# A hybrid attention and mixture-of-experts layer: the stretch from the output projection to the first expert rebuilt, the first group's gather in one piece, the last down projection in its own PSUM bank, the final norm inside the branch

## The chip, the cores and the metric

The kernel runs on one core of a Trainium2 chip. The metric is the device time of one execution in microseconds (us), as the median of the runs of one kernel. Engines are named as in the profile: PE (TensorE), DVE (VectorE), ACT (ScalarE), POOL (GpSimd) and SP (SyncE, which issues most DMA transfers).

## The reference, cut to what matters

256 tokens of width 1024, all float32. Three attention branches give a gated sum `merged`; what follows is where the change lies:

```python
x = layer_norm(DEEPNORM_ALPHA * x + merged @ w_o, ln1_g, ln1_b)      # x1
# router: 4 groups of 4 experts; best group, then its best 2 experts, for every token
p_grp = softmax(t @ w_rg + b_rg);  p_top, g_idx = top_k(p_grp, 1)
sel = take_along_axis((t @ w_re + b_re).reshape(256, 4, 4), g_idx)
pe_top, e_idx = top_k(softmax(sel), 2);  w_tok = p_top * pe_top / sum(pe_top)
for e in range(16):
    h = silu(t @ w1[e]) * (t @ w3[e])          # 1024 -> 512
    out += combine[:, e:e+1] * (h @ w2[e])     # 512 -> 1024
x = layer_norm(DEEPNORM_ALPHA * x + out, ln2_g, ln2_b)
```

## The kernel before

**Stages.** Projections and the three branches fill the first part of the execution. Then come the output projection (8 weight tiles `i`, into four PSUM banks `z[t][half]` for two token tiles `t` of 128 tokens and two column halves), the first layer norm with the router, 16 experts, and the last layer norm with the store.

**First norm and router.** x1 is normalised in place in `xt`, with gamma and beta: `x1_dve` does a half on DVE alone (`L961`, `L963`), `x1_pool` does one by an activation on ACT (`L966`) and a multiplication and an addition on POOL (`L967`, `L968`). x1 is then split into a high part `x1h` (ACT, `L972`) and a remainder `x1l` (`L976`, on DVE or POOL), since PE multiplies in a reduced-precision form of float32 and two products restore the accuracy. The router takes its logits from the sums before normalisation: `pre_T` transposes them (the copies are `L915`), `raw_logits` multiplies, `logits` (`L928` to `L931`) turns the products into `L` with the mean and the reciprocal deviation. DVE ranks the logits by all pairwise comparisons (`L1037` to `L1047`, ties by the mask `lower`), PE counts the places within an expert (`L1055` and around), and DVE makes the one-hot matrices `sel` that pick each expert's up to 64 tokens (`L1123`).

**Gather.** For each group of four experts the chosen tokens are multiplied out of x1h and x1l by `sel` (`L1142`, 8 matmuls for a bank, 4 banks), and ACT or DVE copies a bank to `xg` (`L1144`). For group 0 three banks stand ahead of expert 0's first up step and the fourth between its first and second.

**Experts.** Every expert has 4 up steps (`L1176`; two weight tiles of 512 KB, 8 matmuls), a copy by ACT (`L1181`), transposes, silu and product (`hidden`), and 4 down steps (`L1213`; one tile, 4 matmuls) into one PSUM bank `sd`, whose result goes out by ACT and DVE (`L1219`, `L1220`, the last expert's `L1223`, `L1224`). PE's order is written out in strings: `u` and `d` are steps, `x` is what lies between (the shape of the next hidden layer, and `scatter`, which adds a finished expert's rows into the four accumulators `acc`, `L1235` and `L1243`). The accumulators start from x1 times alpha by PE matmuls with a diagonal matrix (`acc_init`, `L990`).

**Weights.** SP issues one 512 KB transfer for each of the 192 expert tiles, always in order. A tile's target is one of 16 `raw` buffers or a half of a finished region that `W.lend` hands over (`lraw`). The next transfer into a buffer is issued when PE has used the tile in it, so the stream runs ahead as far as buffers are free: 39 tiles are issued before the first up step.

**End.** After the last scatter stands a branch for experts with more than 64 tokens, which is not taken with these inputs. Behind it every engine jumps over that block's code to the last norm (`L1367` to `L1394`: statistics on DVE for token tile 0, sums and squares on ACT for tile 1); four stores of 256 KB follow, issued by SP (`L1384`).

`warm(n)` issues n small matmuls whose result is not used, `WARM` has their numbers.

Of the kernel before, what the change touches and what calls it, by code (L numbers as in the profile page):

```python
# [41 lines left out]
WARM = (5, 8, 19)  # L42
FALLBACK = True
# [146 lines left out]
def tile_block(  # L190
# [159 lines left out]
    lower = consts.tile([128, 4, 4], F32, name="lower")  # L350
    nc.gpsimd.memset(lower, 1.0)
    nc.gpsimd.affine_select(out=lower, in_=lower, pattern=[[1, 4], [-1, 4]], compare_op=OP.is_gt, fill=0.0, base=0,
# [389 lines left out]
    def router_sums():  # L742
        b = bank("sd", None)
        nc.gpsimd.memset(junk, 1.0)
        for k in range(KC):
            nc.tensor.matmul(b[:, 0:40], junk, R["wrg"][:, k].rearrange("p a n -> p (a n)"), start=(k == 0),
                             stop=(k == KC - 1))
        wsum = R["wsum"]
        nc.vector.tensor_copy(wsum, b[:, 0:40].rearrange("p (a n) -> p a n", a=2))
        nc.vector.tensor_add(wsum[:, 1, :], wsum[:, 1, :], R["br"])  # L750
# [117 lines left out]
    def wo_mm(i, t):  # L868
        hi, lo = W.parts(nproj + i)
        hf = (i // 2) % 2  # L870
        for kk in range(2):
            k = 4 * (i // 4) + 2 * (i % 2) + kk
            ts = slice(t * 128, t * 128 + 128)
            for n, (w, a) in enumerate(((hi, R["oh"]), (lo, R["oh"]), (hi, R["ol"]))):
                nc.tensor.matmul(z[t][hf], a[:, k, ts], w[:, kk, :], start=(k == 0 and n == 0),
                                 stop=(k == KC - 1 and n == 2))

    class Stats:


        def __init__(self):
            self.st = small.tile([128, 2, 6], F32, name="lnst")
# [3 lines left out]
        def half(self, h, src):  # L886
            nc.vector.bn_stats(self.st[:, h, :], src)  # L887
# [5 lines left out]
        def shift(self):  # L893

            d = small.tile([128, 1], F32, name="shift")
            nc.vector.scalar_tensor_tensor(d, self.mv[:, 0:1], -1.0, self.rs, op0=OP.mult, op1=OP.mult)
            return d

# [3 lines left out]
    def ln1_half(s, t, h):  # L902

        v = xt[:, t, 512 * h:512 * h + 512]
        nc.vector.scalar_tensor_tensor(v, v, ALPHA, z[t][h], op0=OP.mult, op1=OP.add)
        s.half(h, v)
# [3 lines left out]
    def pre_T(t, h):  # L910
        b = bank("sd", (4, 128))
        for i in range(4):
            k = 4 * h + i
            nc.tensor.transpose(b[:, i, :], xt[:, t, k * 128:k * 128 + 128], ident)
        nc.scalar.copy(preT[:, 4 * h:4 * h + 4, t * 128:t * 128 + 128], b)  # L915

    def raw_logits(t, h):

        if h == 0:
            lb[t] = bank("sd", None)  # L920
        for k in range(4 * h, 4 * h + 4):
            nc.tensor.matmul(lb[t][:, 0:20], preT[:, k, t * 128:t * 128 + 128], wrg[:, k, 0, :], start=(k == 0),
                             stop=(k == KC - 1))

    def logits(t, s):

        nrs = small.tile([128, 1], F32, name="nrs")
        nc.vector.tensor_scalar(nrs, s.rs, -1.0, None, op0=OP.mult)  # L928
        q = small.tile([128, 20], F32, name="lq")
        nc.vector.scalar_tensor_tensor(q, wsum[:, 0, :], s.mv[:, 0:1], lb[t][:, 0:20], op0=OP.mult, op1=OP.subtract)  # L930
        nc.vector.scalar_tensor_tensor(L[:, t, :], q, nrs, wsum[:, 1, :], op0=OP.mult, op1=OP.add)  # L931
# [7 lines left out]
    nc.vector.tensor_scalar(junk, ident, ALPHA, None, op0=OP.mult)  # L939
# [13 lines left out]
    s0, s1 = Stats(), Stats()  # L953
    for h in range(2):
        ln1_half(s0, 0, h)
    s0.finish()
    d0, d1 = halves_of(x1[:, 0]), halves_of(x1[:, 1])

    def x1_dve(d, s, h, stage):
        if stage == 0:  # L960
            nc.vector.scalar_tensor_tensor(d[h], d[h], s.mv[:, 0:1], g1[h], op0=OP.subtract, op1=OP.mult)  # L961
        else:
            nc.vector.scalar_tensor_tensor(d[h], d[h], s.rs, b1[h], op0=OP.mult, op1=OP.add)  # L963

    def x1_pool(d, s, h, shift):
        nc.scalar.activation(d[h], d[h], AF.Identity, scale=s.rs, bias=shift)  # L966
        nc.gpsimd.tensor_mul(d[h], d[h], g1[h])  # L967
        nc.gpsimd.tensor_add(d[h], d[h], b1[h])  # L968

    def x1_hi(t, h):  # L970
        hs = slice(512 * h, 512 * h + 512)
        nc.scalar.copy(x1h[:, t, hs], x1[:, t, hs])  # L972

    def x1_lo(t, h, eng):
        hs = slice(512 * h, 512 * h + 512)
        eng.tensor_sub(x1l[:, t, hs], x1[:, t, hs], x1h[:, t, hs])  # L976

    def wo_last(i):
        wo_mm(i, 1)
# [4 lines left out]
    acc = [None, None]  # L984

    def acc_init(t):

        acc[t] = [bank("mm", None) for _ in range(2)]
        for h in range(2):
# [3 lines left out]
    pre_T(0, 1)  # L993
    shift0 = s0.shift()
    wo_last(5)
    x1_pool(d0, s0, 1, shift0)
    pre_T(0, 0)
    x1_dve(d0, s0, 0, 0)
    ln1_half(s1, 1, 0)
    x1_dve(d0, s0, 0, 1)  # L1000
    wo_last(6)
    raw_logits(0, 0)
    raw_logits(0, 1)
    pre_T(1, 0)
    wo_last(7)
    x1_hi(0, 0)
    x1_hi(0, 1)
    x1_lo(0, 1, nc.gpsimd)
    logits(0, s0)
    x1_lo(0, 0, nc.vector)  # L1010
    W.lend(0)
    W.lend(1)
    raw_logits(1, 0)
    warm(WARM[0])
    ln1_half(s1, 1, 1)
    s1.finish()
    pre_T(1, 1)
    raw_logits(1, 1)
# [409 lines left out]
```

## Time and profile before

| | |
|---|---|
| median of 3 runs | 663.99 us (663.24 to 665.48) |
| profiled execution | 665.7 us, of which the span of the trace is 664.0 us |
| mean granted clock of PE | 0.985 |
| busy, share of the span | PE 637.4 us (96%), DVE 350.9 (53%), ACT 282.9 (43%), POOL 40.1 (6%) |
| DMA | 176.59 MB, mean 266 GB/s |
| stream of expert weights | 393 to 395 GB/s in each of the 28th to the 37th of the page's 40 slices |

The span runs from the first to the last instruction or transfer in the trace; the time of the execution is a little longer. Times below are counted from the start of the span. A clock of 1.00 is 2.4 GHz, 0.50 is 1.2 GHz.

### The profile page before, as it was taken

What the parts mean: (1) busy time and instruction counts of PE and PEld (TensorE: products, weight loads), DVE (VectorE), ACT (ScalarE), POOL (GpSimd) and SP (SyncE); (2) the same over time, 40 slices, a digit from 0 to 9 for tenths busy, and PEclk for the clock granted to TensorE, in tenths of its full rate; (3) what the DMA queues carried; (4) which work ended last, traced back from release to release, by engine and by line L of the source; (5) the groups of instructions that cost most, each with busy time, mean ns of one, the idle gap of its engine ahead of it and who ended that gap; (6) DMA issues with size and microseconds to landing.
All of it is one profiled execution on the core that took longest, in us unless ns stands there. A gap on an engine that the chain in (4) does not pass through costs nothing. (4 is left out here: it accounts for less than half of the span.)

```text
span 664.0 us, 9601 instructions
## 1 busy us (share of the span) xinstructions
PE 637.4 (96%) x3645; PEld 463.9 (70%) x3645; DVE 350.9 (53%) x594; ACT 282.9 (43%) x487; POOL 40.1 (6%) x65
## 2 busy tenths in 40 slices
PE   6999999999999999999999999899999999999981
PEld 5899999898998888888998888534434433543320
DVE  4755657679888677776676676711122112111214
ACT  6654445466647555454345453312233223222212
POOL 2000000101001002100000002300000000000001
PEclk9999999999999999999999999899999999999987
DMA  8997444555445556797645768899999999999971
GB/s 271 378 386 271 148 143 156 159 149 169 139 148 173 164 159 201 244 342 276 193 166 185 251 191 280 321 314 394 394 394 394 393 394 395 394 394 394 390 264 68
DMA packets 84294, 176.59 MB, mean 266 GB/s; under 512 B 5856, under 2 KB 8320, under 8 KB 83984
## 3 DMA queue, kind: packets, MB, share of 16 engines
q1 hardware_dynamic: 83216, 172.14, 73.9%
q0 software_dynamic: 1024, 3.76, 1.9%
q8 instruction: 30, 0.49, 0.3%
q14 instruction: 24, 0.20, 0.1%
HBM read 174.83 MB, written 1.05 MB: 265 GB/s over the span
## 5 line engine op out<-in xcount | busy, mean ns | idle before, releaser
L131 DVE TENSOR_TENSOR lo_lo<-raw,hi_hi 128x1024 fp32r<-128x1024 f32 x118 | 144.3, 1224 | 92.4 <-ACT hi_hi L116 91.8
L116 ACT CAST hi_hi<-raw 128x1024 fp32r<-128x1024 f32 x118 | 123.2, 1047 | 127.7 <-PE mm L401 54.9
L388 PE MATMUL mm<-xh,hi_hi 128*128 128x256 f32 x320 | 91.8, 287 | 0.0
L388 PE MATMUL mm<-xh,lo_lo 128*128 128x256 f32 x320 | 90.5, 283 | 0.0
L388 PE MATMUL mm<-xl,hi_hi 128*128 128x256 f32 x320 | 90.5, 283 | 0.0
L1220 DVE SCALAR_TENSOR_TENSOR y_5b<-sd,cring,y_5b 64x512 fp32r<-64x512 f32 x30 | 22.5, 750 | 114.8 <-ACT y_5b L1219 114.8
L1176 PE MATMUL sd<-raw,xg 128*64 128x512 f32 x212 | 67.2, 596 | 0.0
L401 PE MATMUL mm<-hi_hi,xh 128*128 128x512 f32 x160 | 64.1, 401 | 0.0
L401 PE MATMUL mm<-hi_hi,xl 128*128 128x512 f32 x160 | 62.5, 391 | 0.0
L401 PE MATMUL mm<-lo_lo,xh 128*128 128x512 f32 x160 | 62.5, 390 | 0.0
L388 PEld LDWEIGHTS mm<-xh,hi_hi 128*128 128x128 f32 x320 | 61.3, 192 | 0.6
L388 PEld LDWEIGHTS mm<-xl,hi_hi 128*128 128x128 f32 x320 | 61.3, 192 | 0.1
L388 PEld LDWEIGHTS mm<-xh,lo_lo 128*128 128x128 f32 x320 | 61.3, 192 | 0.0
L1176 PE MATMUL sd<-lraw,xg 128*64 128x512 f32 x156 | 50.9, 596 | 0.9 <-ACT scratch L1181 0.9
L1181 ACT COPY scratch<-sd 128x512 f32<-128x512 f32 x16 | 9.4, 586 | 81.1 <-PE sd L1176 81.1
L1176 PEld LDWEIGHTS sd<-raw,xg 128*64 128x64 f32 x212 | 19.2, 137 | 29.2 <-issue 24.2
L401 PE MATMUL mm<-hi_hi,fh 128*128 128x512 f32 x96 | 37.9, 394 | 0.0
L401 PE MATMUL mm<-hi_hi,fl 128*128 128x512 f32 x96 | 37.5, 390 | 0.0
L401 PE MATMUL mm<-lo_lo,fh 128*128 128x512 f32 x96 | 37.4, 390 | 0.0
L401 PEld LDWEIGHTS mm<-hi_hi,xl 128*128 128x128 f32 x160 | 30.0, 188 | 6.5
L401 PEld LDWEIGHTS mm<-hi_hi,xh 128*128 128x128 f32 x160 | 30.1, 188 | 5.7
L401 PEld LDWEIGHTS mm<-lo_lo,xh 128*128 128x128 f32 x160 | 30.1, 188 | 5.5
(355 smaller groups left out, 1128.4 us busy)
## 6 DMA issues: line engine op xcount, KB each, us to landing
raw<-in_w_dram SPq DMA_DIRECT2D x80, 512.0 KB, 10.5
raw<-in_w_in_dram SPq DMA_DIRECT2D x75, 512.0 KB, 3.7
lraw<-in_w_dram SPq DMA_DIRECT2D x56, 512.0 KB, 10.6
raw<-in_w_branch_dram SPq DMA_DIRECT2D x24, 512.0 KB, 4.4
lraw_hi<-in_w_dram SPq DMA_DIRECT2D x18, 512.0 KB, 10.6
lraw_lo<-in_w_dram SPq DMA_DIRECT2D x17, 512.0 KB, 10.6
raw<-in_w_mem_kv_dram SPq DMA_DIRECT2D x14, 512.0 KB, 9.4
raw<-in_w_o_dram SPq DMA_DIRECT2D x5, 512.0 KB, 4.4
```

Source lines behind the costliest of these rows:

```text
L116: self.nc.scalar.copy(self.hl[j][0], self.raw[j])
L131: self.nc.vector.tensor_sub(lo, self.raw[j], hi)
L388: nc.tensor.matmul(p, w[:, kk, cs], a[:, k, :], start=(k == 0 and i == 0 and c % 2 == 0), stop=(k == KC - 1 and i == 2), skip_group_check= ...
L401: nc.tensor.matmul(p, a[:, k, ts], w[:, kk, :], start=(k == 0 and i == 0), stop=(k == KC - 1 and i == 2))
L1176: nc.tensor.matmul(p[64 * m:64 * m + 64, :], x, w[:, kk, :], start=(q == 0 and kk == 0), stop=(q == 3 and kk == 1), skip_group_check=True)
L1181: nc.scalar.copy(r, p)
L1220: nc.vector.scalar_tensor_tensor(y[64:128, m], p[rs], c[rs], y[0:64, m], op0=OP.mult, op1=OP.subtract)
```

## The change

- The first norm stops at (x1 - mean) / deviation. `normal` does it on ACT alone, x1h and x1l hold that value, and gamma and beta are applied at the eviction of the gather (`gather_out`: two 128x256 activations for a bank, or two DVE operations for one bank of group 0), in every group.
- The accumulators are the banks of the output projection themselves, written by DVE (`acc_init`, two 512-wide operations for each of four halves) between the up steps of expert 0; the four PE matmuls go. The hand-over of region `5a` to the weight stream moves from the router into `acc_row(0)`, behind up step 0.
- The last weight tile of the output projection is multiplied in two column halves, with statistics for each 256 columns; ranking has two pairwise operations in place of four; the mean's part of the logits has its own operation ahead of the reciprocal deviation.
- All four gather banks of group 0 stand ahead of expert 0; the count matmuls follow them.
- The last down projection has the PSUM bank that the up steps use.
- The last norm is a function, called in both arms of the branch; the usual arm falls through. Its stores are issued by ACT.

```diff
-WARM = (5, 8, 19)
+WARM = (20, 8)
...
+    def normal(t, s):
+        d = small.tile([128, 1], F32, name="shift")
+        nc.scalar.activation(d, s.mv[:, 0:1], AF.Copy, scale=s.rs)
+        nc.scalar.activation(d, d, AF.Copy, scale=-1.0)
+        for v in halves_of(xt[:, t]):
+            nc.scalar.activation(v, v, AF.Identity, scale=s.rs, bias=d)
...
+    def acc_init(t, h):
+        v = xt[:, t, 512 * h:512 * h + 512]
+        nc.vector.scalar_tensor_tensor(v, v, ALPHA, g1[h], op0=OP.mult, op1=OP.mult)
+        nc.vector.scalar_tensor_tensor(acc[t][h], b1[h], ALPHA, v, op0=OP.mult, op1=OP.add)
...
-            nc.tensor.matmul(acc[t][h], junk, x1[:, t, 512 * h:512 * h + 512], start=True, stop=True)
...
-    acc_init(0)
-    W.lend("5a", 1)
-    x1_dve(d1, s1, 1, 0)
-    shift1 = s1.shift()
-    x1_pool(d1, s1, 0, shift1)
-    logits(1, s1)
-    x1_hi(1, 0)
-    warm(WARM[1])
...
-    nc.vector.tensor_tensor(eq, vj, vi, op=OP.is_equal)
-    nc.vector.tensor_tensor(gt, vj, vi, op=OP.is_gt)
-    nc.vector.tensor_mul(eq, eq, lower[:, None, :, :].to_broadcast([128, 10, 4, 4]))
-    nc.vector.tensor_add(gt, gt, eq)
+    nc.vector.tensor_sub(gt, vj, vi)
+    nc.vector.tensor_tensor(gt, gt, least[:, None, :, :].to_broadcast([128, 10, 4, 4]), op=OP.is_gt)
...
+    def gather_out(b, key, i, eng=None):
...
+            if eng is nc.vector:
+                nc.vector.tensor_scalar(o, b[:, kk], g, c, op0=OP.mult, op1=OP.add)
+            else:
+                nc.scalar.activation(o, b[:, kk], AF.Identity, scale=g, bias=c)
...
-        p = bank("sd", None, 1)
+        p = bank("sd", None, 1 if stacked else 0)
...
-    x1_lo(1, 0, nc.vector)
-    x1_dve(d1, s1, 1, 1)
-    batch_gather(0, 0)
-    x1_hi(1, 1)
-    x1_lo(1, 1, nc.gpsimd)
-    batch_gather(0, 1)
+    for i in range(2):
+        normal_lo(1, i)
+    for i, n in enumerate((2, 3, 1, 2)):
+        b = bank("sd", (2, 256), n)
+        gather_mm(b, 0, i)
+        gather_out(b, 0, i, (nc.scalar, nc.vector)[i == 1])
...
+    def acc_row(t):
+        for i in range(2):
+            acc_init(t, i)
+        if t == 0:
+            W.lend("5a", 1)
...
-    for q, f in enumerate((weights_2, weights_3, lambda: acc_init(1), None)):
-        if q < 2:
-            batch_gather(0, 2 + q)
+    for q, todo in enumerate(((acc_row, 0), (weights_1, weights_2), (weights_3,), (acc_row, 1))):
         j += step(j, q)
...
-        nc.sync.dma_start(out[0, 128 * t:128 * t + 128, 512 * h:512 * h + 512], v)
+            nc.scalar.dma_start(out[0, 128 * t:128 * t + 128, 512 * h:512 * h + 512], v)
...
+    with tc.If(most <= SLOTS, preferred_fallthrough_block=True) as usual:
+        last_norm()
+    with usual.Else():
+        overflow()
+        last_norm()
```

On DVE, at the end of the router's chain, from the statistics of the second token tile to the one-hot matrices; before:

```order
L961 SCALAR_TENSOR_TENSOR xt_5b<-xt_5b,lnmv,ln_2_3218 128x512
L896 SCALAR_TENSOR_TENSOR shift<-lnmv,lnrs 128x1
L928 TENSOR_SCALAR nrs<-lnrs 128x1
L930 SCALAR_TENSOR_TENSOR lq<-route,lnmv,sd 128x20
L931 SCALAR_TENSOR_TENSOR L<-lq,nrs,route 128x20
L1037 TENSOR_TENSOR wide_D<-L 128x160
L1038 TENSOR_TENSOR scratch<-L 128x160
L1039 TENSOR_TENSOR wide_D<-wide_D,lower 128x160
L1040 TENSOR_TENSOR scratch<-scratch,wide_D 128x160
L1042 TENSOR_REDUCE rank<-scratch 128x40
L1044 TENSOR_SCALAR goh<-rank 128x8
L1047 SCALAR_TENSOR_TENSOR Am<-rank,goh 128x16 x2
```

and in the changed kernel, whose line numbers are its own:

```order
L522 TENSOR_SCALAR lnrs<-lnmv 128x1
L929 SCALAR_TENSOR_TENSOR lq<-route,lnmv,sd 128x20
L933 SCALAR_TENSOR_TENSOR L<-lq,lnrs,route 128x20
L1033 TENSOR_TENSOR scratch<-L 128x160
L1034 TENSOR_TENSOR scratch<-scratch,least 128x160
L1036 TENSOR_REDUCE rank<-scratch 128x40
L1038 TENSOR_SCALAR goh<-rank 128x8
L1040 SCALAR_TENSOR_TENSOR Am<-rank,goh 128x32
```

The 512-wide normalisation, the two 128x1 operations, two of the pairwise operations and one of the two for `Am` are gone.

On PE, from the second half of group 0's gather into expert 0's up steps; before:

```order
L1142 MATMUL sd<-sel,x1h_3977 128x256 x2
L1142 MATMUL sd<-sel,x1l_3978 128x256 x2
L1176 MATMUL sd<-raw,xg_4305 64x512 x4
L1142 MATMUL sd<-sel,x1h_3977 128x256 x2
L1142 MATMUL sd<-sel,x1l_3978 128x256 x2
L1142 MATMUL sd<-sel,x1h_3977 128x256 x2
L1142 MATMUL sd<-sel,x1l_3978 128x256 x2
L1176 MATMUL sd<-lraw_3151,xg_4305 64x512 x4
L1176 MATMUL sd<-raw,xg_4305 64x512 x4
L990 MATMUL mm<-xt_5b,junk 128x512 x2
L1176 MATMUL sd<-raw,xg_4305 64x512
```

and in the changed kernel, where the gather is `L1131`, the count `L1263` and an up step `L1181`:

```order
L1131 MATMUL sd<-sel,x1h_3977 128x256 x2
L1131 MATMUL sd<-sel,x1l_3978 128x256 x2
L1263 LDWEIGHTS ones
L1263 MATMUL sd<-Am,ones 128x16
L1263 LDWEIGHTS ones
L1263 MATMUL sd<-Am,ones 128x16
L1181 MATMUL sd<-raw,xg_4290 64x512 x4
L1181 MATMUL sd<-lraw_3151,xg_4290 64x512 x4
L1181 MATMUL sd<-raw,xg_4290 64x512 x5
```

The matmuls of the gather and of the accumulators that stood between the up steps are gone from there (an x4 of the up steps is a half step of the trace's x8).

On ACT, from the last scatter to the end; before, the last norm and nothing else:

```order
L1330 UNCONDITIONAL_BRANCH
L1367 ACTIVATE scr_10338,dss<-mm 128x512 x2
L1389 ACTIVATE scr_10338,drs<-mm,shift 128x512
L1383 ACTIVATE f_10337<-f_10337,lnrs 128x512
L1391 ACTIVATE scr_10338,drs<-mm,shift 128x512
L1424 UNCONDITIONAL_BRANCH
```

and in the changed kernel, where it stands right behind the branch on `counts`, with the overflow block's code after it:

```order
L1228 ACTIVATE y_5525<-sd,cring 128x512
L1418 TENSOR_LOAD counts
L1419 COMPARE_AND_BRANCH
L1383 ACTIVATE scr_5565,dss<-mm 128x512 x2
L1405 ACTIVATE scr_5565,drs<-mm,shift 128x512
L1399 ACTIVATE f_5564<-f_5564,lnrs 128x512
L1401 DMA out_dram<-f_5564 128x512
L1407 ACTIVATE scr_5565,drs<-mm,shift 128x512
L1401 DMA out_dram<-f_5564 128x512 x3
L1419 UNCONDITIONAL_BRANCH
```

The first store stands ahead of the second squared activation (`L1407`, before `L1391`), the other three behind it; the jump over the overflow block is now the last instruction.

## Rows read from the trace of the kernel before

**Rows 1.** Windows: us; busy PE, PEld, DVE, ACT, POOL (count); PEclk, DMA share, GB/s.

```profile
428.00:434.00 6.00, 5.23 (x29) 2.73 (x31) 3.82 (x20) 2.38 (x5) 0.95 (x2) 1.00 0.26 82
434.00:446.00 12.00, 10.92 (x51) 3.96 (x48) 0.67 (x4) 1.34 (x3) 0.00 (x0) 1.00 0.98 336
460.00:480.00 20.00, 20.00 (x104) 8.80 (x105) 1.92 (x3) 4.47 (x8) 0.00 (x0) 1.00 1.05 394
644.00:647.00 3.00, 3.00 (x10) 0.72 (x6) 0.00 (x0) 0.00 (x0) 0.00 (x0) 0.50 0.02 5
```

**Rows 2.** SP's timeline, 420 to 434: start us, us, engine, line, out<-in, count.

```profile
422.31 0.38 SPq L87 DMA_DIRECT2D lraw_5a<-in_w_dram  x1
431.52 0.89 SPq L87 DMA_DIRECT2D raw<-in_w_dram  x2
```

**Rows 3.** Tile view of lraw, 630 to 664: the stream's last issues.

```profile
L91 SPq DMA_DIRECT2D lraw<-in_w_dram x4: 328/328/328, 633.9 to 635.9; - x4
...
DMA to landing us min/median/max: 5.3/5.3/5.3
```

**Rows 4.** PE's timeline, the last down projection (bracket: idle before, releaser).

```profile
642.95 1.08 PE L1213 MATMUL sd<-lraw_hi,scratch 128*64 128x512 f32 x4 [3.10 <-DVE y_5b L1220]
643.85 1.80 PE L1213 MATMUL sd<-lraw_lo,scratch 128*64 128x512 f32 x4
645.44 2.86 PE L1213 MATMUL sd<-lraw,scratch 128*64 128x512 f32 x8
```

**Rows 5.** DVE's timeline, 416 to 425: statistics, logits, ranking, one-hot.

```profile
416.31 0.69 DVE L887 BATCH_NORM_STATS2 lnst<-xt_5b 128x6 f32<-128x512 f32 x1
...
418.55 0.16 DVE L896 SCALAR_TENSOR_TENSOR shift<-lnmv,lnrs 128x1 f32<-128x1 f32 x1 [0.45 <-POOL lnrs L524]
...
419.04 0.24 DVE L931 SCALAR_TENSOR_TENSOR L<-lq,nrs,route 128x20 f32<-128x20 f32 x1
...
419.56 0.32 DVE L1038 TENSOR_TENSOR scratch<-L 128x160 f32<-128x160 f32 x1
419.79 1.39 DVE L1039 TENSOR_TENSOR wide_D<-wide_D,lower 128x160 f32<-128x160 f32 x1
421.21 1.31 DVE L1040 TENSOR_TENSOR scratch<-scratch,wide_D 128x160 f32<-128x160 f32 x1
...
423.91 0.76 DVE L1123 TENSOR_TENSOR sel<-slot,place 128x256 fp32r<-128x256 f32 x2
```

**Rows 6.** DVE's slowest 512-wide operation of the first norm, from its timeline.

```profile
410.27 1.84 DVE L961 SCALAR_TENSOR_TENSOR xt_5a<-xt_5a,lnmv,ln 128x512 f32<-128x512 f32 x1 [0.94 <-PE sd L914]
```

**Rows 7.** POOL's timeline, 420 to 423: x1's addition of beta.

```profile
421.08 1.26 POOL L968 TENSOR_TENSOR xt_5b<-xt_5b,ln 128x512 f32<-128x512 f32 x1
```

**Rows 8.** PE's timeline, gather of group 0 and up steps of expert 0.

```profile
425.79 0.40 PE L1142 MATMUL sd<-sel,x1l 128*128 128x256 f32 x2
...
426.97 0.84 PE L1142 MATMUL sd<-sel,x1h 128*128 128x256 f32 x2
...
429.56 1.94 PE L1176 MATMUL sd<-raw,xg 128*64 128x512 f32 x8
...
434.33 1.89 PE L1176 MATMUL sd<-raw,xg 128*64 128x512 f32 x8
436.15 1.98 PE L990 MATMUL mm<-xt_5b,junk 128*128 128x512 f32 x4
438.07 0.64 PE L1176 MATMUL sd<-raw,xg 128*64 128x512 f32 x1
...
440.71 0.64 PE L1176 MATMUL sd<-lraw,xg 128*64 128x512 f32 x1 [0.71 <-ACT scratch L1181]
```

**Rows 9.** Windows: the router's chain, same columns as Rows 1.

```profile
418.00:422.00 4.00, 4.00 (x11) 1.78 (x11) 3.44 (x9) 0.81 (x1) 2.80 (x3) 0.59 1.02 387
```

**Rows 10.** The chain that ended last: start us, us, what it was.

```profile
650.74 2.17 issue
...
656.30 1.76 POOL f L1384
```

More of the change, by code (lines that the diff above doesn't have):

```diff
@@ L891, in finish, with ln1_part @@
             rsqrt_eps(self.rs, self.mv[:, 1:2])
[L893 to L897, printed above, removed]
     def halves_of(a):
         return [a[:, 0:512], a[:, 512:1024]]
[L902 to L906, printed above, removed]
+    def ln1_part(s, t, i, n=512):
+        v = xt[:, t, n * i:n * i + n]
+        h, c = divmod(n * i, 512)
+        nc.vector.scalar_tensor_tensor(v, v, ALPHA, z[t][h][:, c:c + n], op0=OP.mult, op1=OP.add)
+        for p in range(n * i, n * i + n, s.cols):
+            s.part(p // s.cols, xt[:, t, p:p + s.cols])
@@ L925, in logits @@
     def logits(t, s):
[L927 to L931, printed above, removed]
+        nc.vector.scalar_tensor_tensor(L[:, t, :], lq[t], s.rs, wsum[:, 1, :], op0=OP.mult, op1=OP.add)
@@ L1053, in tile_block @@
     nc.tensor.matmul(pb[:, 16:32], before, Af[:, 1, :], start=False, stop=True)
[L1054 to L1056 removed]
+    warm(WARM[1])
     place = consts.tile([128, NT, NE], F32, name="place")
@@ L1136, in batch_gather @@
             B[key, "xg"] = region((4, 2)[key % 2], [128, KC, 4 * SLOTS], name="xg")
[L1137 removed]
         b = bank("sd", (2, 256), 2 + i % 2)
[L1139 to L1144 removed]
+        gather_mm(b, key, i)
+        gather_out(b, key, i)
     c_ring = st_tile([128, 4], "cring")
@@ L1248, in tile_block @@
     banks["sd"] = ctx.enter_context(tc.tile_pool(name="psum_experts", bufs=1, space=PSUM))
-    x1_lo(1, 0, nc.vector)
-    x1_dve(d1, s1, 1, 1)
-    batch_gather(0, 0)
-    x1_hi(1, 1)
-    x1_lo(1, 1, nc.gpsimd)
-    batch_gather(0, 1)
+    B[0, "xg"] = region(4, [128, KC, 4 * SLOTS], name="xg")
+    for i in range(2):
[4 more added lines that the diff above has]
+        gather_out(b, 0, i, (nc.scalar, nc.vector)[i == 1])
+    b = bank("sd", None, 3)
+    for t in range(NT):
+        nc.tensor.matmul(b[:, 0:NE], ones, Af[:, t, :], start=(t == 0), stop=(t == 1))
+    nc.vector.tensor_copy(cnt_f[:, 0:NE], b[:, 0:NE])
     late_t = reg.tile([128, 192], F32R, name="late", tag="dist")
@@ L1355, in tile_block @@
-    ln2 = E["ln2"]
-    f = region(6, [128, NT, D], name="f")
-    scr = region(7, [128, 512], name="scr")
-    sm = small.tile([128, 2], F32, name="dss")
-    sq = small.tile([128, 2], F32, name="drs")
-    nm = small.tile([128, 1], F32, name="shift")
-    rs1 = small.tile([128, 1], F32, name="nrs")
-    s0 = Stats()
-    for h in range(2):
-        s0.half(h, acc[0][h])
-        nc.scalar.activation(scr, acc[1][h], AF.Copy, accum_out=sm[:, h:h + 1])
-    s0.finish()
-    def part(t, h):
-        return f[:, t, 512 * h:512 * h + 512]
@@ L1399, in tile_block, with overflow @@
-    scale(1, 1, nc.vector)
+    def overflow():
+        for e in range(NE):
+            cnt = nc.values_load(counts[0:1, e:e + 1], min_val=0, max_val=T)
+            with tc.If(cnt > SLOTS, preferred_fallthrough_block=False):
+                key = 5 + 2 * e
+                batch_select(key, [(e, SLOTS * i) for i in range(4)])
+                for i in range(4):
+                    batch_gather(key, i)
+                for i in range(0, 4, 2):
+                    batch_back(key, i, (e, e))
+                for i in range(1, 4):
+                    wq = Weights(nc, (raw_p, region), ups[e] + downs[e], range(12))
+                    for _ in range(12):
+                        wq.load()
+                    step = up(wq, key, i, r)
+                    for q in range(4):
+                        step(2 * q, q)
+                    hm, turn, gate, product = hidden(r)
+                    turn()
+                    gate()
+                    product()
+                    y = y_tile("5b")
+                    step = down(wq, hm, B[key, "c", i], y)
+                    for k in range(4):
+                        step(8 + k, k)
+                    scatter(y, B[key, "ST", i])
```

252 lines of the change are left out of this document (120 added, 132 removed).

## The prediction, made before the changed kernel ran

> **What bounds the kernel now.** I read the page first, then the windows of busy time stage by stage, then the engines' timelines where two stages meet, and last the chain that ended last. Up to the output projection the change touches nothing, so only the time behind about 405 us counts. In the windows of the expert stage PE is busy 20.00 of 20 us while the DMA engines are busy all the time at 394 GB/s [rows 1]. Two chains thus run side by side, and the reader has to see how close they are. The PE chain starts with the first up step at 429.56 [rows 8]. The last down projection waits 3.10 us for a bank and then starts at 642.95, with 0.90 us from its first to its second step [rows 4]: without the wait PE would have done the step before at 639.85, and would start the last of the four steps at 639.85 + 3 x 0.90 = 642.5. The stream's last tile is issued at 635.9 and lands 5.3 us later, at 641.2 [rows 3]. So the weights lead by 1.3 us at the very end, and a saving on PE beyond that is worth nothing unless the stream comes earlier too.
>
> The stream has a hole. The last transfer ahead of the experts goes out at 422.31, the next only at 431.52, when up step 0 has set buffers free [rows 2]. Between 428 and 434 the DMA moves 82 GB/s, and 336 in the 12 us behind, where it otherwise moves 394 [rows 1]. That is (394 - 82)/394 x 6 = 4.75 us plus (394 - 336)/394 x 12 = 1.77 us, 6.5 us of transfer time lost. A tile of 512 KB takes 524/394 = 1.33 us.
>
> **1. Router to first up step: -4.4 us.** L of the second token tile starts at 419.04 [rows 5]. Before it leave half of the last statistics (0.69) and half of the equally long addition ahead of them (together about 0.65, as they now cover 256 columns at the end), and the shift that stands behind the wait for POOL at 418.55 with its 128x1 neighbour (0.2); the mean's part moves into that wait (0.2). I take 1.0. The pairwise stage had two ordinary operations of 0.32 and two of 1.39 and 1.31 [rows 5]. The two slow ones run while POOL multiplies and adds, 1.26 for the addition at 421.08 [rows 7]; POOL's two operations go. Two operations of 0.32 remain, so 0.32 + 0.32 + 1.39 + 1.31 becomes 0.64: -2.7, and one operation for `Am` and the count's copy leave too. `sel` was ready at 423.91 + 0.76 = 424.67 [rows 5], now at about 421.0. ACT must in the same time, from about 418.5 on, make x1 and x1h out of the statistics, four 512-wide operations behind two short ones; these rows show none of ACT's, so I bound one by DVE's of the same width, 0.69 [rows 5] to 1.84 [rows 6]: ready at 418.5 + 4 x 0.69 + 0.2 = 421.5, near the same, or at 426 at the worst. From 425.79 to 426.97 ten gather matmuls took 1.18 us [rows 8], 0.118 each; 32 in one piece take 3.8, less what can begin on the first half. First up step at about 425.1 in place of 429.56. If DVE's two pairwise operations keep the slow price, it is 427.1; if ACT's activations take 1.84 each, 428. I take the low end, since 0.69 is the usual price and 1.84 one row's.
>
> **2. Inside expert 0's up steps: -3.1 us.** From the first up step to the next expert's is 440.71 - 429.56 = 11.15 us [rows 8]. In it are one gather bank, 8 matmuls, 1.15 in the timeline's grouping with its edges, and the accumulators' four matmuls, 438.07 - 436.15 = 1.92 [rows 8]. Both leave: 8.1 remain, that is three steps of 436.15 - 434.33 = 1.82 and 2.64 behind 438.07. The accumulators are now eight DVE operations of 512, about 0.7 each (upper end 1.84 [rows 6]), in all 5.6, between weights and the product of expert 0. In their place DVE loses none of its other work; as the first half of it lies ahead of the router weights, these are ready about 434, and the product is needed at about 437. PE does not wait for either. The gather's two activations of 256 columns cost ACT some 0.2 more for a bank than the one copy, hidden behind PE's matmuls. Sum on PE: -7.5; with the bounds of step 1, -4.6 to -8.
>
> **3. The stream: -5.2 us.** The 82 GB/s of the window from 428 say that 492 KB moved in it, about one tile: what was in hand ran out near 428, and restarted with the issue at 431.52. Now region `5a` is handed over behind up step 0, so 38 tiles instead of 39 are in hand and the stream runs dry 1.33 us sooner, near 427. Up step 0 ends near 425.1 + 1.9 = 427.0 [rows 8], and the first data need another us. So about 1.3 us remain lost in place of 4.75. The 1.77 us behind it go: four up steps of 1.82 in a row free two tiles each, that is 2.67 us of transfer for 1.82 of PE. 6.5 - 1.3 = 5.2; last tile at 641.2 - 5.2 = 636.0. Bounds: first up step at 426 (-4.3), and no hole at all with the earlier end (-6).
>
> **4. Last down: -11.3 us at its end.** With a bank of its own it follows the projection before it. By the PE chain its last step would start at 642.5 - 7.5 = 635.0, by the stream at 636.0: the stream decides. The last step ends about 1 us later, 637.0. Before it ended at 645.44 + 2.86 = 648.30 [rows 4]: PE stood still for 3.10 us and then had a clock of 0.50 [rows 1], at which the remaining three steps took twice the time. The copies of the projection before end about 635.4, and nothing waits for them any more but a scatter behind the last down. The tail behind the last down (two evictions, scatter) is 650.74 - 648.30 = 2.4, unchanged: 639.4.
>
> **5. The end: -0.3 us.** From the scatter's end to the span's it takes 664.0 - 650.74 = 13.3 us. Of these 2.17 are issue [rows 10], with every engine idle: the jump over the overflow block. In the usual arm the norm follows directly: -2.2. The jump at the end lies beside the landing of the last store. Against it stands the first store on ACT's queue, ahead of the second squared activation. A store waits for POOL's addition, 656.30 to 658.06 [rows 10], and ACT with it; the square used to run in that time, and the sums of token tile 1, its scale and both its stores come behind it: 1.76, and 0.1 for the issue. -2.2 + 1.9 = -0.3. Branch and register load stand on both sides.
>
> Sum: 664.0 - 11.3 - 0.3 = 652.4 as span, -11.6. The profiled execution took 665.7, so 1.7 lie around the span, which stays; the median of the runs, 663.99, is 1.7 less than it. 663.99 - 11.6 = 652.4.
>
> **The rivals.** (a) The stream keeps its hole: if the four up steps free buffers later than thought, or the transfers behind the hole do not catch up, the last tile lands at 641.2, step 4 gives 642.2 in place of 637.0, and the time is 652.4 + 5.2 = 657.6. For it: a tile fewer is in hand. Against: the first release is 4.4 us earlier. Chance 0.10.
>
> (b) The clock. Between 418 and 422 PE's granted clock is 0.59 [rows 9], the level of 1.2 GHz most of that time, while small transposes and idle waits ran; the gather of before ran at full speed behind 424. The gather now begins at 421. If it and the first up step all run at 1.2 GHz, 3.8 + 1.9 us grow to 11.4; as about a fifth of that is edges and not matmuls, +4.5. The buffers of step 0 come free 4.5 us later, the stream's hole grows by as much, and the last tile with it: 656.9. For half of the stretch it is 654.7; I take 655.8. Chance 0.13.
>
> (c) The jump is only moved. If the span waits for the jump behind the last store's issue, or the arm's code is not at hand either, the 2.17 us come back: 654.6. Both arms hold a norm, and the usual one ends with a jump over the overflow code. For it: the 2.17 us of before were spent at such a place; against: the engines reach the closing jump when the last store has only been issued, and the span waits for its landing anyway. Chance 0.10. The Trainium skill, "Runtime: NRT & Kernel Launch", section "Instruction fetch mechanics", says that a taken branch whose target is not in the current window makes a DMA fetch and stalls the engine; by that rule the fall-through is free of it and the closing jump pays it, and the trace of before agrees with a pause of 2.17 us. No run here yet shows which of the two places costs.
>
> (d) Slower than before: the DVE-written accumulators. They stand in DVE's order between weights and product of expert 0, with PE waiting for the product. To cost 12 us on the path, the eight operations would have to take over 2.2 us each (8 x (2.2 - 0.7) = 12), beyond the slowest row of its kind, 1.84 [rows 6]. Chance 0.03.
>
> The rest, 0.06, is a better end than 650.3: no store blocking (DVE's later half not waiting), or a stream without loss.
>
> **How the numbers follow.** Forecast 0.58, with a range of its own from 650.3 (stream -6, no block behind the store: 652.4 - 0.8 - 1.9 = 649.7 at the best, so 650.3 for most) to 655; (b) 655.8, (c) 654.6, (a) 657.6, (d) over 664. A range from 650.0 to 657.3 leaves out (d), half of (a) and some of the rest, about 0.14. About 0.3% is what a measurement of this kernel can tell from no change, 2 us. Faster: all but (d) and mixtures that meet, 0.95; same 0.02; slower 0.03.
>
> **What would show it.** Step 1: first up step near 425, `sel` near 421, no operation of 1.3 us in the ranking. Step 2: the next expert's up 8.1 us after it. Step 3: the stream's window behind the first up step at more than 300 GB/s; the last tile landing near 636. Step 4: no idle of 3 us ahead of the last down, full clock up to its end, at most a short wait for a tile. Step 5: the first DVE operation directly behind the scatter, and the second squared activation starting only with the end of POOL's addition. The prediction is wrong if PE waits for accumulators or product in expert 0, if the last tile still lands near 641, or if the 2.17 us stand at another place.

## The result, and the profile after

| | before | after |
|---|---|---|
| median | 664.2 us (663.24 to 665.48, 4 runs) | 654.4 us (653.39 to 654.78, 4 runs) |
| ratio | | 0.9849, 95% interval 0.9828 to 0.987 |
| profiled execution, span | 665.7, 664.0 | 653.39, 651.6 |

The changed kernel is 9.8 us faster. The forecast was 652.4 in a range of 650.0 to 657.3, so the time lies in the range, and the saving of 11.6 us was put 1.8 us too high.

**A common zero first.** The two spans differ by 12.4 us, more than the medians. PE's timeline shows why: the first matmul of the output projection, the first place that the change touches, stands in the trace of before and of after at

```profile
389.23 0.39 PE L875 MATMUL mm<-hi_hi,oh 128*128 128x512 f32 x1
```

```profile
386.53 0.39 PE L877 MATMUL mm<-hi_hi,oh 128*128 128x512 f32 x1
```

2.7 us apart, with the same work ahead of them. In the twelve other traces below it lies between 386.5 and 388.5. A part of the difference can be seen near the start: the windows of the first 20 us, of before and then of after (columns as in [rows 1]), have a different granted clock.

```profile
0.00:20.00 20.00, 13.66 (x74) 12.70 (x75) 10.48 (x15) 12.25 (x22) 3.81 (x19) 0.91 0.85 290
```

```profile
0.00:20.00 20.00, 14.11 (x92) 12.96 (x93) 11.26 (x16) 13.21 (x23) 3.70 (x19) 1.00 0.86 294
```

In five of the 14 traces the clock falls to 0.50 for a part of the time between 15 and 21 us (before, e6, after_again, after_third, e7). These five start the output projection latest, at 388.10 to 389.23; the nine without it start it at 386.53 to 388.00. Most of the 2.7 us is thus a difference between executions; whether the first part of before is by itself a little longer, its two traces (389.23, and 388.40 in e6) don't tell. So below every place is given as its distance from that matmul, "from zero":

| us from zero | before | after | moved | forecast |
|---|---|---|---|---|
| first up step | 40.33 | 36.43 | -3.9 | -4.4 |
| first up step of the next expert | 51.48 | 44.23 | -7.3 | -7.5 |
| last weight tile lands | 251.96 | 248.06 | -3.9 | -5.2 |
| last down ends | 259.07 | 249.18 | -9.9 | -11.3 |
| PE's last matmul ends | 261.40 | 251.47 | -9.9 | -11.3 |
| end of the span | 274.77 | 265.07 | -9.7 | -11.6 |

**Router and gather.** DVE's timeline of the changed kernel (start us, us, engine, line, operation, out<-in, shapes, count):

```profile
415.55 0.23 DVE L929 SCALAR_TENSOR_TENSOR lq<-route,lnmv,sd 128x20 f32<-128x20 f32 x1 [0.83 <-PE sd L922]
415.90 0.24 DVE L933 SCALAR_TENSOR_TENSOR L<-lq,lnrs,route 128x20 f32<-128x20 f32 x1
416.18 0.33 DVE L1033 TENSOR_TENSOR scratch<-L 128x160 f32<-128x160 f32 x1
416.53 0.33 DVE L1034 TENSOR_TENSOR scratch<-scratch,least 128x160 f32<-128x160 f32 x1
...
418.20 0.76 DVE L1113 TENSOR_TENSOR sel<-slot,place 128x256 fp32r<-128x256 f32 x2
...
423.16 0.68 DVE L982 SCALAR_TENSOR_TENSOR xt_5a<-xt_5a,ln 128x512 f32<-128x512 f32 x1
423.88 0.70 DVE L983 SCALAR_TENSOR_TENSOR mm<-ln,xt_5a 128x512 f32<-128x512 f32 x1
```

The pairwise operations take 0.33 us, with no POOL work beside them, where two of before took 1.39 and 1.31 [rows 5]. The second of these ended 0.18 us behind POOL's addition [rows 5, rows 7]. No run has the new pair beside POOL's work, so that POOL held the old pair back is argued from these rows and not tested. An accumulator operation takes 0.68 to 0.70, and the eight of them delay nobody: among the waits of PE's matmuls from 405 on there is none for an accumulator.

```profile
engine line waited for: us in total, times, longest us
PE sd L1044 <- DVE Am L1040: 1.1, 1, 1.1
PE sd L1181 <- ACT scratch L1186: 0.7, 1, 0.7
PE sd L914 <- DVE xt_5b L903: 0.5, 1, 0.5
PE sd L1131 <- DVE sel L1113: 0.4, 1, 0.4
PE sd L1158 <- DVE scratch L1205: 0.4, 1, 0.4
```

PE's timeline: the first step of expert 0 and of the next up projection. Their distance is 7.8 us, where it was 11.15 [rows 8].

```profile
422.96 1.94 PE L1181 MATMUL sd<-raw,xg 128*64 128x512 f32 x8
...
430.76 0.64 PE L1181 MATMUL sd<-lraw,xg 128*64 128x512 f32 x1 [0.71 <-ACT scratch L1186]
```

**The stream.** SP's timeline and then the windows (columns as in [rows 1]):

```profile
413.49 3.45 SPq L86 DMA_DIRECT2D lraw<-in_w_dram  x4
424.93 0.89 SPq L86 DMA_DIRECT2D raw<-in_w_dram  x2
425.99 0.34 SPq L86 DMA_DIRECT2D lraw_5a<-in_w_dram  x1
```

```profile
422.00:428.00 6.00, 6.00 (x35) 2.67 (x35) 4.83 (x24) 3.10 (x7) 0.00 (x0) 1.00 0.73 242
428.00:434.00 6.00, 5.29 (x26) 1.49 (x22) 3.25 (x8) 1.36 (x3) 0.00 (x0) 1.00 1.03 379
434.00:446.00 12.00, 11.63 (x62) 4.97 (x62) 3.20 (x12) 5.26 (x12) 0.00 (x0) 1.00 1.04 397
...
632.00:636.00 4.00, 4.00 (x14) 1.27 (x13) 0.76 (x1) 0.91 (x2) 0.00 (x0) 1.00 0.89 346
```

```profile
424.53:426.53 2.00, 2.00 (x12) 0.65 (x10) 1.97 (x11) 0.11 (x1) 0.00 (x0) 1.00 0.32 78
426.53:428.53 2.00, 2.00 (x12) 0.64 (x10) 1.79 (x13) 1.54 (x3) 0.00 (x0) 1.00 0.96 280
```

The hole is still there, but costs (394 - 242)/394 x 6 + (394 - 379)/394 x 6 = 2.5 us in place of 6.5 [rows 1]. The difference, 4.0, is about what the last tile gained (3.9). The first issue behind the hole stands at 424.93; up to 426.53 the stream moves 78 GB/s, and in the two microseconds behind that only 280 where it otherwise moves 394 [rows 1].

**The last down.** The stream's last issues and PE's timeline:

```profile
L90 SPq DMA_DIRECT2D lraw<-in_w_dram x4: 328/328/328, 627.4 to 629.4; - x4
...
DMA to landing us min/median/max: 5.2/5.3/5.3
```

```profile
629.16 1.28 PE L1218 MATMUL sd<-lraw_lo,scratch 128*64 128x512 f32 x4
630.13 1.64 PE L1218 MATMUL sd<-lraw_hi,scratch 128*64 128x512 f32 x4
631.38 1.74 PE L1218 MATMUL sd<-lraw_lo,scratch 128*64 128x512 f32 x4
632.72 2.99 PE L1218 MATMUL sd<-lraw,scratch 128*64 128x512 f32 x8
```

The 3.10 us ahead of the last down, which starts at 630.13, are gone [rows 4]. Its steps begin 1.25 to 1.34 us apart, the time of a tile in the stream, at a granted clock of 1.00 (the window from 632 above): PE follows the tiles, the last of which lands at 629.4 + 5.2 = 634.6, and ends 1.1 us behind it.

**The end.** The chain of the last norm (start us, us, what), and of ACT's timeline the row of the square:

```profile
637.87 1.31 DVE lnst L890 x2
...
640.55 0.66 ACT f L1399
...
641.28 1.76 POOL f L1400
...
643.06 0.38 ACTq L1401
...
643.49 0.07 ACT scr L1407
```

```profile
643.49 0.69 ACT L1407 ACTIVATE scr<-mm,shift 128x512 f32<-128x512 f32 x1 [2.29 <-POOL f L1400]
```

DVE starts the norm as soon as its bank is complete, even before PE's last matmul ends at 638.01, where 2.17 us of issue stood [rows 10]. But the store holds the square back by 2.29 us, and the way from PE's last matmul to the end is 13.6 us, as long as before (13.4).

### The profile page after: what moved, and what is told of

It is laid out like the page before. It is cut to its first block, busy times and chain, and to the rows that moved or that the text cites. A ratio compares the mean times of both kernels' runs of the same rounds, so it can differ in the third digit from the quotient of the medians.

```text
span 651.6 us, 9603 instructions
## 1 busy us (share of the span) xinstructions
PE 629.1 (97%) x3639; PEld 461.5 (71%) x3639; DVE 349.6 (54%) x595; ACT 292.0 (45%) x510; POOL 31.6 (5%) x59
## 4 chain that ended last, share of the span: by engine, by line
PE 95%; DVE 1%; DMA 1%; SPq 1%; ACT 0%; issue 0%; POOL 0%; ACTq 0%; DVEq 0%
PE mm L400 30%; PE mm L387 21%; PE sd L1181 17%; PE sd L1218 9%; PE mm L877 3%; PE sd L1131 2%; PE mm L1240 2%; PE sd L1199 1%; DMA raw<-in_w_mem_kv_dram 1%; PE sd L532 1%; PE sd L533 1%; PE sd L531 1%; PE sd L645 1%; PE sd L922 1%; PE sd L591 1%; PE sd L596 0%
## 5 line engine op out<-in xcount | busy, mean ns | idle before, releaser
L1181 PE MATMUL sd<-raw,xg 128*64 128x512 f32 x224 | 67.1, 595 | 0.0
L1181 PE MATMUL sd<-lraw,xg 128*64 128x512 f32 x156 | 50.9, 596 | 0.7 <-ACT scratch L1186 0.7
L1181 PEld LDWEIGHTS sd<-raw,xg 128*64 128x64 f32 x224 | 19.4, 137 | 31.1 <-issue 25.7
```

Source lines behind the costliest of these rows:

```text
L1181: nc.tensor.matmul(p[64 * m:64 * m + 64, :], x, w[:, kk, :], start=(q == 0 and kk == 0), stop=(q == 3 and kk == 1), skip_group_check=True)
```

## The experiments

All times from zero unless said otherwise; one trace each. PE's first up step, the last tile's landing, PE's last matmul and the end:

| kernel | first up | last tile | PE ends | end | median (runs) |
|---|---|---|---|---|---|
| before | 40.33 | 251.96 | 261.40 | 274.77 | 664.2 to 664.6 in three batches, 663.4 in a fourth |
| after | 36.43 | 248.06 | 251.47 | 265.07 | 654.40 (4) |
| after_again | 36.43 | 247.71 | 251.13 | 264.79 | 655.03 (4) |
| after_third | 36.44 | 247.75 | 251.17 | 264.80 | 654.80 (6) |
| e1 stores by SP | 36.45 | 248.22 | 251.63 | 264.67 | 654.18 (5) |
| e2 last down, shared bank | 36.43 | 248.01 | 252.81 | 266.43 | 656.43 (6) |
| e3 gather interleaved | 35.31 | 247.61 | 251.08 | 264.71 | 654.12 (5) |
| e5 norm behind the branch | 37.93 | 249.03 | 252.45 | 267.67 | 655.99 (4) |
| e6 before, own bank | 41.59 | 252.90 | 257.69 | 271.10 | 659.58 (4) |
| e7 first store behind the square | 37.93 | 249.52 | 252.93 | 264.99 | 652.69 (4) |
| e9 accumulators first | 36.44 | 246.94 | 250.36 | 264.04 | 654.88 (4) |
| e10 = e7 + e9 | 37.93 | 248.54 | 251.96 | 263.90 | 653.17 (6) |
| e11 = e10 + more small matmuls | 36.44 | 246.99 | 250.39 | 262.40 | 651.71 (6) |
| e11, second trace | 37.42 | 247.81 | 251.22 | 263.38 | 652.40 (1) |

The changed kernel ran beside e1, e2 and e3 (655.03) and beside e10 and e11 (654.80), but not beside e5, e6, e7 and e9, whose batch has the before of 663.4. By medians the changed kernel lies 9.6 to 9.8 below the before of its batch, e5 7.4, e7 10.7 and e9 8.5.

**The changed kernel again (after_again, after_third).**

> The changed kernel once more, beside the others on one chip. In the two traces so far the first matmul of the output projection starts at 389.23 before and at 386.53 after, although nothing ahead of it differs in work; theory A: these 2.7 us are a difference between executions of the first loads, so this run's trace may start that stage anywhere from 386 to 390, and from there to the end of the span it takes 265.1 us again (within 0.6). Theory B: the change itself makes the first part 2.7 us faster, and the stage starts at 386.5 again. Time 653.5 to 655 by both.

> The changed kernel again, as the standard for the two combinations of this batch. Two kinds of trace have shown up: with the clock of PE at 1.00 through the gather the first up step starts 36.4 us behind the first matmul of the output projection, with 0.50 for part of it at 37.9. This trace shows one of the two; from that matmul to the end 264.8 to 265.1 or 265.8 to 266.5.

Zero lies at 388.1 in both traces, and 264.8 follow. So the first part varies by itself, as theory A says, and the change is worth 274.8 - 264.9 = 9.9 us from zero, as the medians say.

**e2: the bank undone in the changed kernel.**

```diff
-        p = bank("sd", None, 1 if stacked else 0)
+        p = bank("sd", None, 1)
```

> The last down projection shares the bank with the one before it again, all else as changed. Theory: PE stands still for 3.1 us ahead of it (630.4 to 633.5), while the last tiles land, and its last step ends at 633.5 + 3.6 = 637.1 in place of 635.7 if the clock stays up (+1.4), or at 633.5 + 5.35 = 638.9 with the clock of 0.50 that the trace of before shows there (+3.2). Rival, that the stream alone sets the end and hides the wait: +0.3 at most.

PE's timeline has the wait back:

```profile
633.69 1.08 PE L1218 MATMUL sd<-lraw_hi,scratch 128*64 128x512 f32 x4 [3.06 <-DVE y_5b L1225]
634.60 1.03 PE L1218 MATMUL sd<-lraw_lo,scratch 128*64 128x512 f32 x4
635.46 1.89 PE L1218 MATMUL sd<-lraw,scratch 128*64 128x512 f32 x8
```

PE ends 1.3 to 1.7 us later than in the three traces of the changed kernel, as set down for a clock that stays up, and the median is 1.4 above that of the same batch. The clock stays up in this trace (two steps in 1.89, not 2.86); two of the six runs were at 659.3 and 659.6, with a mean granted clock of 0.985 and 0.981 where the other four have 0.989 to 0.992; where the clock fell in them no trace shows. Of the 3.06 us only about half reaches the end; the other half falls into time in which PE, in the changed kernel, waits for tiles.

**e6: the bank alone in the kernel before.** The same edit the other way round.

> The kernel before with one edit: the last down projection has the bank of the up steps. Theory: the 3.1 us of PE's wait and the clock of 0.50 behind it go; the stream's last tile lands as before, 252.0 us behind the first matmul of the output projection, and PE's chain (253.3 + 0.9 = 254.2) sets the end of the last down in place of 259.1: 4.9 us less in all, about half of the whole change. Rival: the clock or the stream holds it, at most 3 us less.

```profile
640.16 1.03 PE L1213 MATMUL sd<-lraw_hi,scratch 128*64 128x512 f32 x4
641.01 1.03 PE L1213 MATMUL sd<-lraw_lo,scratch 128*64 128x512 f32 x4
641.87 1.89 PE L1213 MATMUL sd<-lraw,scratch 128*64 128x512 f32 x8
```

From zero the end comes 3.7 us earlier, and the medians of the batch differ by 3.8 (ratio 0.9946, 0.9926 to 0.9967). In this trace the first up step is 1.26 later than in that of before; the granted clock was 0.55 and 0.59 in the four us from 422.4, where the gather runs. From the first up step to PE's last matmul it is 216.10 against 221.07, 4.97 less. So by the traces the working was right: 3.10 of it is the wait, and 1.75 the last down itself, which takes 5.35 us in that one trace of before, at a clock of 0.50 for most of it [rows 1, rows 4], and 3.60 here. By the medians the bank is worth 3.8, between the wait alone and both.

**e3: the gather interleaved again.**

```diff
+    gather_0(0, 2)
+    gather_0(1, 3)
...
         j += step(j, q)
+        if q < 2:
+            gather_0(2 + q, 1 + q)
+        if q == 1:
+            counts_mm()
```

> Gather banks 2 and 3 of group 0 (with the count matmuls) stand behind up steps 0 and 1 again instead of ahead of them, all else as changed; PE's work is the same. Theory S, the weight stream sets the end of the experts, and the hole in it lasts until up step 0 frees buffers: the first up step starts 1.5 to 1.9 us earlier, the first release too, and the whole is 1.2 to 1.9 us faster than the changed kernel. Theory P, PE's chain sets the end: 0 within 0.4. Rival: the first up step then waits for ACT's eviction of the first bank, and nothing is won.

```profile
422.90 2.64 PE L1181 MATMUL sd<-raw,xg 128*64 128x512 f32 x8
```

```profile
421.00:423.00 2.00, 2.00 (x12) 1.78 (x12) 0.22 (x1) 1.02 (x2) 0.00 (x0) 0.50 1.06 393
```

The number was missed: the first up step came 1.1 us earlier, but PE's clock was 0.50 there, the step took 2.6 us instead of 1.8, and SP's first issue behind it came only 0.4 us earlier (425.57 - 387.59 = 37.98 from zero, before it 424.93 - 386.53 = 38.40). The end is the same, which by the numbers set down would speak for theory P; the medians, 654.12 beside 655.03, lie in overlapping runs (652.00 to 655.30 and 654.62 to 655.54). But the condition of theory S, an earlier release, was not there. What the trace does show: the next expert's first up step stands at 46.46 from zero, 2.2 us later than in the changed kernel, and PE's last matmul is not a bit later. A PE chain that set the end would have been 2.2 us late. That speaks for theory S, and the last tile, 0.1 to 0.5 us earlier, moved with the release.

**e9: the accumulators first.**

```diff
+    acc_row(0)
     for i, n in enumerate((2, 3, 1, 2)):
         b = bank("sd", (2, 256), n)
         gather_mm(b, 0, i)
-        gather_out(b, 0, i, (nc.scalar, nc.vector)[i == 1])
+        gather_out(b, 0, i)
...
-    for q, todo in enumerate(((acc_row, 0), (weights_1, weights_2), (weights_3,), (acc_row, 1))):
+    for q, todo in enumerate(((weights_1,), (weights_2,), (weights_3,), (acc_row, 1))):
```

> DVE writes token tile 0's accumulators, and region 5a goes to the weight stream, ahead of group 0's gather instead of behind up step 0; ACT evicts all four banks. PE's work and order are the same. Theory S, the weight stream and its hole set the end: the tile for 5a is issued near 36.6 us behind the first matmul of the output projection in place of 39.5, fills 1.33 us of the hole, and the last tile lands 1.0 to 1.3 us earlier, at 246.6 to 247.0, the whole as much faster. Rival: the gather's evictions or the router weights come later, PE waits, and it is the same or up to 1 us slower.

```profile
422.92 0.38 SPq L86 DMA_DIRECT2D lraw_5a<-in_w_dram  x1
424.96 0.89 SPq L86 DMA_DIRECT2D raw<-in_w_dram  x2
```

PE's work and its start are those of the changed kernel (36.44), only the tile for `5a` goes out at 36.4 from zero instead of 39.5. The last tile lands 0.8 to 1.1 us earlier, and PE and the end follow by 0.8 to 1.1. Expected were 1.0 to 1.3. The same edit is in e10 and e11: e11's trace without a fall of the clock has the last tile at 246.99, and e10's, with the first up step at 37.93, at 248.54 where e5 and e7 have 249.03 and 249.52. Together with e3 this shows it for the traces: in the changed kernel the stream and its hole set the end of the experts, not PE. The medians do not show a gain. The trace is of e9's fastest run (652.28), the other three took 654.63 to 655.30, and by its median e9 lies 8.5 us below the before of its batch, 1.1 to 1.3 less than the changed kernel does. The intervals overlap (0.9858 to 0.9899 for e9, 0.9833 to 0.9897 for after_again), so the worth of this edit alone in the time of a run stays open.

**e5: the norm behind the branch.**

```diff
-    with tc.If(most <= SLOTS, preferred_fallthrough_block=True) as usual:
-        last_norm()
-    with usual.Else():
-        overflow()
-        last_norm()
+    with tc.If(most > SLOTS, preferred_fallthrough_block=False):
+        overflow()
+    last_norm()
```

> The last norm stands behind the branch again (the overflow block alone is in it and is jumped over), the stores still by ACT, all else as changed. Theory: the jump ahead of the norm comes back with its 2.2 us of idle engines, and the closing jump, which in the changed kernel takes ACT from 647.8 to 650.7 while the last store lands at 649.9, gives back less than 0.3: from PE's last matmul to the end 13.6 + 1.9 to 2.2 = 15.5 to 15.8. Rival, that the jump is only moved to the end: 13.3 to 13.9.

```profile
639.69 2.21 issue
641.90 1.31 DVE lnst L890 x2
```

The pause is back at its old place and size. From PE's last matmul to the end it is 15.2 us against 13.6, a little under the 15.5 to 15.8 set down and far over the rival's 13.9: 1.6 of the 2.2 are lost, 0.6 come back at the other end. Two things differ there. The changed kernel's ACT leaves its closing branch at 647.8 and shows its next record at 650.7, 0.8 us behind the last store's landing at 649.9; in after_again, e7, e10 and e11, which have that branch too, the same stretch takes 2.8 to 3.3 us. And in e5 the stores land after 2.0 to 2.2 us, in the changed kernel after 2.2 to 2.5. How much of the 0.6 is the branch's stays open. The jump is not merely moved, but it may not be free either. The Trainium skill ("Runtime: NRT & Kernel Launch", section "Instruction fetch mechanics") says that a taken branch to a target outside the current window stalls its engine; the trace agrees at both places, 2.21 us ahead of the norm here and 2.9 us on ACT's closing branch there. POOL passes the same branch at 644.8 and shows its next record at 645.0; which targets lie outside the window no run shows.

**e1 and e7: the first store out of the square's way.** e1 has `nc.sync.dma_start` for the four stores, e7 this:

```diff
         nc.scalar.activation(scr, acc[1][1], AF.Square, bias=nm, accum_out=sq[:, 1:2])
+        store(0, 0)
```

> The four stores go back to SP's queue, all else as changed. Theory: the first store on ACT's queue holds the second squared activation back until POOL's addition ends (641.20 to 643.49 in the trace), and the end of the norm with it: the square starts 2.3 us earlier, the whole takes 2.0 to 2.4 us less than the changed kernel. Rival: the stores themselves start or land later by SP, or the closing jump of SP's queue costs: gain 0 to 0.7.

> The first store stays on ACT's queue but is issued behind the second squared activation, all else as changed. Theory: the square no longer waits for POOL's addition, so the last DVE operation ends about 2.3 us earlier as with the stores on SP. The end follows by 1.9 to 2.3 us if the last store and ACT's closing jump behind it set the end (13.6 to 11.3 to 11.7 behind PE's last matmul); if something else at the end does, as with the stores on SP's queue, where 1.1 us more passed between the barrier's steps, 0.5 to 1.0.

In both the square runs directly behind the activation ahead of it, and from PE's last matmul to DVE's last operation it is 7.0 us, 2.3 to 2.4 less than in the changed kernel (9.3). The way from PE's last matmul to the end became 0.6 shorter in e1, as its rival had it, and 1.5 to 1.6 in e7, between the two values set down. By the medians e7 lies 10.7 below the before of its batch, about 1 us more than the changed kernel. Where the rest went: the four stores now come within 2.3 to 2.6 us of each other and land later. The tile view of the output in the changed kernel and in e7:

```profile
L1401 ACTq DMA_DIRECT2D out_dram<-f x4: 338/360/478, 643.1 to 647.4; - x4
...
DMA to landing us min/median/max: 2.2/2.4/2.5
```

```profile
L1405 ACTq DMA_DIRECT2D out_dram<-f x4: 338/436/612, 646.4 to 648.5; - x4
...
DMA to landing us min/median/max: 2.3/3.0/3.5
```

That is up to 1 us. In e1 about 1 us more passes on SP in the closing barrier, between two of its steps behind the stores (649.7 to 651.2, where the changed kernel has 650.5 to 651.0); why, is open.

**e10 and e11: the combinations.**

```diff
-WARM = (20, 8)
+WARM = (34, 13)
```

> Two edits together: the accumulators of token tile 0 (and region 5a) ahead of the gather, and the first store behind the second squared activation. Theory: they act in different places (1.0 us of the stream, 1.5 us of the end) and add up: 2.0 to 2.6 us below the changed kernel in the same batch, median 651.5 to 652.5; from the first matmul of the output projection to the end 262.3 to 262.8, or 1.0 to 1.5 more where the clock falls in the gather. Rival: the earlier end of the experts is eaten by the end of the kernel, gain under 1.2.

> As the combination, and the small matmuls without use that fill PE's waits for the ranking and for the one-hot matrices go from 20 and 8 to 34 and 13. Theory C, the clock of 0.50 in the gather follows PE's idle 1.07 and 0.37 us there: with these waits filled, PE's clock stays at 1.00 through the gather, first up step at 36.4 again, and the runs spread less, median 0.3 to 0.8 below the combination. Rival: the clock falls whatever PE does there, or in the busy stretch too; first up step at 37.9 in a part of the executions, same median.

> A second trace of the kernel with more small matmuls: by theory C first up step at 36.4 us behind the first matmul of the output projection and clock 1.00 from 30 to 38 us behind it; by its rival 37.9 in about every second trace.

e10 is 1.6 us below the changed kernel of its batch by the medians (expected 2.0 to 2.6), and its trace, one with the clock of 0.50 in the gather, ends where it was expected for that case (263.9). e11 is the fastest kernel: 651.71 (650.74 to 653.06) beside 654.80, 3.1 us below the changed kernel and 12.8 below before (ratio 0.9805, 0.9779 to 0.9831). Theory C, though, falls by the second trace. PE's small matmuls fill the wait, and the clock falls in them:

```profile
415.00:417.00 2.00, 2.00 (x26) 2.00 (x25) 0.95 (x6) 1.13 (x4) 0.56 (x1) 0.91 1.02 396
417.00:419.00 2.00, 2.00 (x22) 2.00 (x21) 1.30 (x5) 2.00 (x4) 0.39 (x1) 0.50 1.05 397
```

The slow stretch lies earlier there and costs 1.0 us at the first up step. That e11's median is 1.5 below e10's is measured; whether the filled waits did it is not settled by two traces. Its runs spread over 2.3 us, e10's over 1.3, where theory C wanted less.

## Why the prediction was right, and where it was off

**1, router to first up step: right in mechanism.** -3.9 for -4.4. The pairwise operations cost what was put for them (0.33 for 0.32), and the slow ones of before are gone. The half microsecond is missing ahead of them: L of the second token tile came 0.4 us earlier (29.37 from zero for 29.81) instead of the 1.0 that was taken, since the operation ahead of it waits 0.83 us for PE's router products. ACT's eviction of a gather bank costs 0.4 us more than the copy (1.02 for 0.59), not 0.2, and hides as forecast.

**2, inside expert 0's up steps: right.** 7.8 us for the 8.1 of the working, since an up step takes 1.72 to 1.77 us and not 1.82. The accumulators by DVE hide, as forecast, and rival (d) falls: 0.7 us an operation, no wait.

**3, the stream: the step that was mis-sized.** "About 1.3 us remain lost" became 2.5, so the last tile gained 3.9 instead of 5.2, and since the stream decides, as step 4 said, this 1.3 is in the end. The first release came where it was put (38.4 from zero; 427.0 in the time of before is 37.8), only 0.6 later, and the stream takes longer than the assumed microsecond to come back: from 1.6 to 3.6 us behind the release it moves 280 GB/s, not 394. e9's trace confirms it from the other side: one tile more in the hole brings the last tile 0.8 to 1.1 forward.

**4, the last down: right.** Bound by the last tile, 1.1 us behind it, no fall of the clock; it ends 9.9 earlier, about 11.3 less the 1.3 of step 3. The fall of the clock in before made the last three steps 1.6 times as long (4.45 us [rows 4] for 2.75 in e6), not twice. e6 and e2 give the bank's part: 3.8 by the medians and 5.0 by the traces in the kernel before, where PE's chain decided, but 1.4 in the changed one, since there the stream hides the rest. The parts of this change do not add up one by one.

**5, the end: both mechanisms right, their sizes not.** The jump's 2.2 us go, but by e5 only 1.6 of them reach the end: up to 0.6 returns at the closing branch, which was put at nothing, so rival (c) is true for a quarter at most. The square loses 2.3 instead of 1.9, of which by e7 1.5 to 1.6 reach the end. The two about cancel; the measured sum is +0.2 where -0.3 was written. "Every engine idle" holds for half of the old pause only: in e5, where it is back, ACT starts the norm at 640.79, DVE at 641.90.

**The rivals on the clock.** (b) exists, but not in every execution: of the twelve traces with the changed router five have the clock of 0.50 at a place where it costs (e3, e5, e7, e10, e11's second trace), and e1 has it where it costs nothing. In e5, e7 and e10 the first up step is 1.5 us later (37.93 for 36.43), not 4.5. The reading of [rows 9] behind this rival was off: what ran at that clock was not mainly small transposes and waits, since PE is busy 4.00 of 4.00 us there, but the accumulators' four large matmuls:

```profile
418.57 3.66 PE L990 MATMUL mm<-xt_5a,junk 128*128 128x512 f32 x4
```

(a) falls: the hole shrank.

**The zero.** The saving was worked out against one trace and taken off the median of the runs. That trace had a long first part, which belongs to the execution, and in its last down a clock of 0.50. Whether this second one is regular in the kernel before, one trace cannot tell: e2's trace has the same wait without the fall.

## What to carry to other kernels

When two chains run side by side, write both of them down to the same last instruction before pricing an edit: here PE saved 7.3 us up to the second expert, the stream only 3.9, and the stream set the end. A gap in a stream of weights is closed by what is issued ahead of it or early in it, not by a faster consumer behind it: handing over one buffer 3 us earlier brought the last tile about 1 us forward without any work removed (in the traces; the medians of e9 do not show it), while 2.2 us on PE behind the gap moved nothing (e3). Put a transfer that waits for another engine behind the work of its queue's own engine, and compare traces from the first place that the change touches: what lies ahead of it varied by 2.7 us.

## What was not expected of the hardware

- PE's granted clock fell to 0.50 for some microseconds between the output projection and the first up steps in some executions and not in others: of the seven traces with the changed kernel's own order there (after three times, e1, e2, e5, e7) in e1, e5 and e7, and also where the waits were filled (0.50 in the window at 417 of e11's second trace, with PE busy 2.00 of 2 us).
- Four stores of 256 KB issued within 2.2 us landed after 2.3 to 3.5 us, spread over 4.3 us after 2.2 to 2.5.
- ACT needed 2.9 us from its closing branch (647.8) to its next record (650.7), and 2.8 to 3.3 in four more traces, beside the 2.2 us of pause at the jump of before; POOL needed 0.2 at the same branch.
- In five of 14 traces PE's granted clock fell to 0.50 between 15 and 21 us, and these five reached the output projection latest.
